# A two-layer hybrid decoder trunk on one core: weight blocks in tiles of 1024 columns instead of 512

## The chip, the cores and the metric

The kernel runs on one core of one Trainium2 chip. Its metric is the device time of one execution in microseconds (us), taken as the median of several runs. A core has TensorE for matrix products (PE in the rows, its weight loads PEld), VectorE (DVE), ScalarE (ACT), GpSimd (POOL) and SyncE (SP), which here issues all transfers between the chip's memory (HBM) and SBUF. Each engine works through its own instructions in the order in which the program lists them, and waits where an operand or a buffer isn't ready.

## The reference

The sequence has 512 tokens of width 1024, in float32; the trunk has two layers, each with three residual steps.

```python
for l in range(DEPTH):
    ff = swiglu(rms_norm(x, g[l, 0]), ffn_w1[l, 0], ffn_w3[l, 0], ffn_w2[l, 0])   # D_FF = 2816
    x = x + 0.5 * rms_norm(ff, g[l, 1])
    h = rms_norm(x, g[l, 2])
    p = h @ w_in[l]                       # 3336 columns (and 32 of w_in_vres in layer 1)
    y_a = rwkv7_time_mix(p[..., :1024])   # delta rule, 4 heads of 64
    y_b = s5_mix(p[..., 1024:1280])       # complex diagonal state space
    y_c = gated_deltanet_mix(p[..., 1280:3336])   # delta rule, 4 heads of 128
    x = x + rms_norm(concat(y_a, y_b, y_c) @ w_out[l], g[l, 3])
    ff = swiglu(rms_norm(x, g[l, 4]), ffn_w1[l, 1], ffn_w3[l, 1], ffn_w2[l, 1])
    x = x + 0.5 * rms_norm(ff, g[l, 5])
```

Here `swiglu(z, w1, w3, w2)` is `(silu(z @ w1) * (z @ w3)) @ w2`.

## The kernel before

The tokens are worked in two halves of 256. A list of steps in `run` names the stages: `A` and `B` are the two feed-forward networks, `P` the input projection, `M` the token mixers, `O` the output projection, followed by the layer and the half (`B10` is the second network of layer 1 on the first half); small letters begin a stage early or finish it late. A mixer of one half (`M`) is written next to a feed-forward stage of the other half, and a scheduler that works from a model of the engines' times decides how the instructions of neighbouring stages are interleaved on each engine. The order is fixed when the program is built.

Matrix products with weights are done to nearly float32 precision with fp32r operands: the activations and the weights are each split in a high part (a rounded copy) and a low part (the rest), and three products are added (`mm3`, lines 245 to 247). So each weight takes this path: a transfer by SP into a tile `raw`, a copy by ACT into `whi` (line 226), a subtraction by DVE into `wlo` (line 227), and then matmuls. A *block* is 1024 columns of weights on 128 partitions (512 KB): the 8 x 128 columns of one step of `w1`, `w3` or `w_in`, or 2 x 512 columns of one step of `w2` or `w_out`. `weight` takes a block in two tiles of 512 columns; `raw` has 6 buffers, `whi` and `wlo` have 4 each. The last columns of `w_in` (`gate`) come in four blocks of 2 x 520 (layer 0) or 2 x 552 columns (layer 1), a tile for each of the two.

A feed-forward step `f` of 22 (`up`, then `down` of the step before) uses a block of `w1` and one of `w3`, 24 matmuls of 256 columns each into the tile `ph`, and a block of `w2`, 12 matmuls of 512 columns into `acc`. A tile of 512 columns thus feeds 12 or 6 matmuls. Some `w_out` blocks (`plain` in `outmul`) are not split: TensorE reads them from `raw` in float32 (line 1355). The gains of the norms after a stage (`gain`) also use `raw` buffers, two per norm, from their transfer to the products at line 338.

At the start of a stage `prenorm` scales the rows into `xs` (line 299), TensorE turns them (`xt`, line 309), and for each of 8 slices of 128 columns ACT writes `hth` and DVE writes `htl` (lines 317 and 318), which the first matmuls of the stage need slice by slice. The mixers use small transfers on the same SP queue: `lv` and `lx` (lines 1243 and 1285) are the tables of the S5 mixer, and `scr` and `blk` (lines 568 and 571) rearrange the matrices to be inverted.

Of the kernel before, what the change touches and what calls it, by code (L numbers as in the profile page):

```python
# [12 lines left out]
F32 = mybir.dt.float32  # L13
F32R = mybir.dt.float32r
# [6 lines left out]
P = 128  # L21
# [20 lines left out]
class Trunk:  # L42
# [171 lines left out]
    def weight(self, src, n, w, src2=None, w2=0):  # L214

        nc = self.nc
        m = n // 2
        his, los = [], []
        for z in range(2):
            q = self.wts.tile([P, m, w + w2], F32, tag="raw", name=self.n("raw"), bufs=6)  # L220
            nc.sync.dma_start(out=q[:, :, 0:w], in_=src[:, z * m:z * m + m])
            if w2:
                nc.sync.dma_start(out=q[:, :, w:w + w2], in_=src2[:, z * m:z * m + m])
            hi = self.wts.tile([P, m, w + w2], F32R, tag="whi", name=self.n("whi"), bufs=4)
            lo = self.wts.tile([P, m, w + w2], F32R, tag="wlo", name=self.n("wlo"), bufs=4)
            nc.scalar.activation(hi, q, AF.Copy)  # L226
            nc.vector.tensor_tensor(lo, q, hi.bitcast(F32), ALU.subtract)  # L227
            his.append(hi)
            los.append(lo)
        return [his[k // m][:, k % m] for k in range(n)], [los[k // m][:, k % m] for k in range(n)]  # L230
# [93 lines left out]
    def postnorm(self, accs, h, gain, half, chunks=(0, 1)):  # L324
        with self.tc.high_priority(100):
            self.postnorm_(accs, h, gain, half, chunks)

    def postnorm_(self, accs, h, gain, half, chunks):
        nc = self.nc
        for i in chunks:  # L330
            x = self.x[2 * h + i]
            ss = self.sm([P, 2], "pss")
            for d in range(2):
                junk = self.fw.tile([P, 512], BF16, tag="junk", name=self.n("junk"), bufs=1)
                nc.scalar.activation(junk, accs[i][d], AF.Square, scale=(2.0 if half else 1.0) * D ** -0.5, accum_out=ss[:, d:d + 1])
            r = self.rstd2(ss, (4.0 if half else 1.0) * EPS, "po")
            for d in range(2):
                nc.vector.tensor_tensor(accs[i][d], accs[i][d], gain[d], ALU.mult)
            for d in range(2):
                e = slice(d * 512, (d + 1) * 512)  # L340
                nc.vector.scalar_tensor_tensor(x[:, e], accs[i][d], r, x[:, e], ALU.mult, ALU.add)

    def gain(self, l, i):
        ts = []
        for d in range(2):
            t = self.wts.tile([P, 512], F32, tag="raw", name=self.n("gain"), bufs=6)
            self.nc.sync.dma_start(out=t, in_=self.io["norm_gain"][l, i][d * 512:(d + 1) * 512].partition_broadcast(P))
            ts.append(t)
        return ts


    def up(self, S, f):
# [981 lines left out]
    def outmul(self, l, k, mixT, plain, chunks, accs):  # L1334

        nc = self.nc
        e = slice(chunks[0] * P, (chunks[-1] + 1) * P)
        src = self.io["w_out"][l][k * P:(k + 1) * P, :].rearrange("p (d e) -> p d e", d=2)
        if plain:
            ws = []  # L1340
            for d in range(2):
                w = self.wts.tile([P, 512], F32, tag="raw", name=self.n("raw"), bufs=6)
                nc.sync.dma_start(out=w, in_=src[:, d])
                ws.append(w)
        else:
            a = self.fw.tile([P, HALF], F32R, tag="gh", name=self.n("mh"), bufs=2)
            b = self.fw.tile([P, HALF], F32R, tag="gl", name=self.n("ml"), bufs=2)
            nc.scalar.activation(a[:, e], mixT[:, k, e], AF.Copy)
            nc.vector.tensor_tensor(b[:, e], mixT[:, k, e], a[:, e].bitcast(F32), ALU.subtract)
            wh, wl = self.weight(src, 2, 512)  # L1350
        for i in chunks:
            s = slice(i * P, (i + 1) * P)
            for d in range(2):
                if plain:
                    nc.tensor.matmul(accs[i][d], mixT[:, k, s], ws[d], start=k == 0, stop=k == KT - 1)  # L1355
                else:
                    self.mm3(accs[i][d], a[:, s], b[:, s], wh[d], wl[d], k == 0, k == KT - 1)
# [120 lines left out]

# [9 lines left out]
```

## Time and profile before

| | |
|---|---|
| median of 3 runs | 2284.42 us (2283.87 to 2288.77) |
| the profiled execution, its own time | 2297.84 us |
| its span, first to last instruction | 2296.1 us |
| TensorE busy with matmuls | 2235.3 us, 97% of the span |
| VectorE busy | 1686.1 us, 73% |
| ScalarE busy | 1190.5 us, 52% |
| GpSimd busy | 173.8 us, 8% |
| mean granted clock of TensorE | 0.988 |

A span is what the profiler saw between the first and the last instruction; the execution's own time is a little longer. Busy time is the union of an engine's instructions; an engine that is busy nearly all of the span sets the time, and what the others do matters where it makes that engine wait. The granted clock is 1.00 at 2.4 GHz and 0.50 at 1.2 GHz.

### The profile page before, as it was taken

The page shows a single profiled execution, that of the slowest core. Times are in us where ns is not written, and L with a number is a line of the kernel's source. Part 1 is how long each engine was busy: PE and PEld are TensorE (multiplying, and loading weights), DVE is VectorE, ACT ScalarE, POOL GpSimd, SP SyncE. Part 2 cuts the span into 40 slices and gives each one's busy share as a digit, 9 for nine tenths or more (in the row PEclk, how much of TensorE's full clock was granted, in tenths as well). Part 3 has the DMA queues.
Part 4 walks back from the last instruction along what each step waited for, and adds up shares of the span by engine and source line. Part 5 has one row for each costly group of instructions (what it writes and reads, how often), then busy time and mean ns, then how long its engine had stood idle before and what let it go on. Part 6 is the DMA issues. An engine that isn't in the chain of part 4 may idle for free.

```text
span 2296.1 us, 44446 instructions
## 1 busy us (share of the span) xinstructions
PE 2235.3 (97%) x15800; PEld 2048.1 (89%) x15800; DVE 1686.1 (73%) x3771; ACT 1190.5 (52%) x2513; POOL 173.8 (8%) x380
## 2 busy tenths in 40 slices
PE   8999999999999999999999999999999999999998
PEld 7998999997978999799999999899978889987997
DVE  6597885966877866859776688686777678667665
ACT  5455754444645544655555566445455444445554
POOL 2032000001100000202200010000010000001000
PEclk9999999999999999999999999999999899999999
DMA  6776755646756644576666676475477366445665
GB/s 205 192 209 188 190 164 159 201 142 176 186 160 185 192 136 148 170 204 206 200 178 188 187 195 169 127 214 161 143 195 200 107 193 187 137 126 182 189 186 155
DMA packets 604963, 403.67 MB, mean 176 GB/s; under 512 B 63306, under 2 KB 534340, under 8 KB 604740
## 3 DMA queue, kind: packets, MB, share of 16 engines
q1 hardware_dynamic: 604740, 400.82, 60.8%
q8 instruction: 124, 2.03, 0.4%
q14 instruction: 99, 0.81, 0.1%
HBM read 387.09 MB, written 13.63 MB: 175 GB/s over the span
## 4 chain that ended last, share of the span: by engine, by line
PE 87%; DMA 4%; DVE 4%; POOL 2%; issue 2%; ACT 1%; SPq 0%; DVEq 0%; ACTq 0%; POOLq 0%
PE ph L246 13%; PE ph L247 13%; PE ph L245 13%; PE acc L245 7%; PE acc L246 7%; PE acc L247 7%; PE pp L247 4%; PE pp L245 4%; PE pp L246 4%; PE acc L1355 1%; POOL Q L1196 1%; DVE wlo L227 1%; DMA raw<-in_w_out 1%; PE pk L760 1%; PE pb L764 1%
## 5 line engine op out<-in xcount | busy, mean ns | idle before, releaser
L226 ACT ACTIVATE whi<-raw 128x512 fp32r<-128x512 f32 (+2 forms) x1296 | 813.4, 632 | 857.4 <-PE ph L246 407.8
L227 DVE TENSOR_TENSOR wlo<-raw,whi 128x512 fp32r<-128x512 f32 (+2 forms) x1296 | 892.2, 692 | 427.0 <-ACT whi L226 408.9
L245 PE MATMUL ph<-hth,whi 128*128 128x256 f32 x2464 | 702.5, 285 | 6.8 <-DVE htl L318 2.9
L247 PE MATMUL ph<-hth,wlo 128*128 128x256 f32 x2464 | 703.5, 286 | 4.3 <-DVE wlo L227 4.1
L246 PE MATMUL ph<-htl,whi 128*128 128x256 f32 x2464 | 703.7, 286 | 2.0 <-DVE htl L318 1.8
L245 PEld LDWEIGHTS ph<-hth,whi 128*128 128x128 f32 x2464 | 468.1, 190 | 20.9 <-issue 5.5
L246 PEld LDWEIGHTS ph<-htl,whi 128*128 128x128 f32 x2464 | 467.2, 190 | 14.9 <-issue 3.9
L247 PEld LDWEIGHTS ph<-hth,wlo 128*128 128x128 f32 x2464 | 468.2, 190 | 11.5 <-DVE wlo L227 7.1
L246 PE MATMUL acc<-wlo,gh 128*128 128x512 f32 x704 | 277.3, 400 | 0.0
L247 PE MATMUL acc<-whi,gl 128*128 128x512 f32 x704 | 270.0, 397 | 0.3 <-DVE gl L371 0.3
L245 PE MATMUL acc<-whi,gh 128*128 128x512 f32 x704 | 257.4, 401 | 0.1
L247 PEld LDWEIGHTS acc<-whi,gl 128*128 128x128 f32 x704 | 132.0, 189 | 29.6 <-issue 0.7
L246 PEld LDWEIGHTS acc<-wlo,gh 128*128 128x128 f32 x704 | 132.4, 189 | 23.5 <-issue 1.0
L245 PEld LDWEIGHTS acc<-whi,gh 128*128 128x128 f32 x704 | 130.6, 190 | 22.7 <-issue 1.0
L370 ACT ACTIVATE gh<-gu 128x256 fp32r<-128x256 f32 x176 | 71.7, 407 | 58.6 <-DVE gu L364 57.7
L245 PE MATMUL pp<-hth,whi 128*128 128x256 f32 x352 | 99.6, 283 | 2.5 <-ACT whi L226 2.1
L245 PE MATMUL ph<-hx,whi 128*128 128x256 f32 x352 | 99.7, 283 | 0.9 <-DVE gu L364 0.9
L246 PE MATMUL ph<-hx,whi 128*128 128x256 f32 x352 | 99.5, 283 | 0.0
L247 PE MATMUL ph<-hx,wlo 128*128 128x256 f32 x352 | 99.4, 282 | 0.0
L247 PE MATMUL pp<-hth,wlo 128*128 128x256 f32 x352 | 98.7, 282 | 0.7 <-DVE wlo L227 0.7
L246 PE MATMUL pp<-htl,whi 128*128 128x256 f32 x352 | 98.6, 281 | 0.1
L245 PE MATMUL pp<-hx,whi 128*128 128x256 f32 x352 | 98.5, 281 | 0.0
(491 smaller groups left out, 3400.4 us busy)
## 6 DMA issues: line engine op xcount, KB each, us to landing
raw<-in_ffn_w SPq DMA_DIRECT2D x1056, 256.0 KB
raw<-in_w_in SPq DMA_DIRECT2D x176, 256.0 KB
raw<-in_w_out SPq DMA_DIRECT2D x96, 256.0 KB
raw<-in_w_in SPq DMA_DIRECT2D x32, 260.0 KB
gain<-in_norm_gain SPq DMA_DIRECT2D x28, 256.0 KB
lx<-s5w SPq DMA_DIRECT2D x16, 384.0 KB
lv<-s5w SPq DMA_DIRECT2D x16, 256.0 KB
x<-in_x SPq DMA_DIRECT2D x4, 512.0 KB
```

Of the source, the lines that this page charges most:

```text
L226: nc.scalar.activation(hi, q, AF.Copy)
L227: nc.vector.tensor_tensor(lo, q, hi.bitcast(F32), ALU.subtract)
L245: mm(out, lh, rh, start=start, stop=False)
L246: mm(out, lh, rl, start=False, stop=False)
L247: mm(out, ll, rh, start=False, stop=stop)
L370: nc.scalar.activation(gh, u, AF.Copy, scale=0.5)
L760: nc.tensor.matmul(pk[:, j], ka[q, j, c], ar[q, j, c], start=True, stop=True)
L764: nc.tensor.matmul(pb[:, j], be[q, j, c], ar[q, j, c], start=True, stop=True)
L1196: nc.gpsimd.tensor_scalar(Q[z][hp][q, :, j, 16 * g:16 * g + 16], cur[z][q, 4 * hp:4 * hp + 4], 1.0 - 2 * z, 0.0, ALU.mult, ALU.add)
L1355: nc.tensor.matmul(accs[i][d], mixT[:, k, s], ws[d], start=k == 0, stop=k == KT - 1)
```

## The change

`weight` takes a block of up to 1024 columns as one tile, with one transfer, one copy and one subtraction, instead of two of each. `raw` gets 5 tiles of 1024 columns (before 6 of 512), `whi` and `wlo` 3 each (before 4 of 512). Blocks of `gate` have more than 1024 columns and are still halved; each half of 520 or 552 columns then takes a whole buffer. The gain of a norm and a plain block of `w_out` become one tile with one transfer. A scratch area that the program reserves in SBUF for descriptors of transfers is set to 1024 bytes; no transfer of this kernel is issued by GpSimd.

```diff
     def weight(self, src, n, w, src2=None, w2=0):
...
-        m = n // 2
+        m = n if n * (w + w2) <= 1024 else n // 2
         his, los = [], []
-        for z in range(2):
-            q = self.wts.tile([P, m, w + w2], F32, tag="raw", name=self.n("raw"), bufs=6)
+        for z in range(n // m):
+            q = self.wts.tile([P, m, w + w2], F32, tag="raw", name=self.n("raw"), bufs=5)
             nc.sync.dma_start(out=q[:, :, 0:w], in_=src[:, z * m:z * m + m])
             if w2:
                 nc.sync.dma_start(out=q[:, :, w:w + w2], in_=src2[:, z * m:z * m + m])
-            hi = self.wts.tile([P, m, w + w2], F32R, tag="whi", name=self.n("whi"), bufs=4)
-            lo = self.wts.tile([P, m, w + w2], F32R, tag="wlo", name=self.n("wlo"), bufs=4)
+            hi = self.wts.tile([P, m, w + w2], F32R, tag="whi", name=self.n("whi"), bufs=3)
+            lo = self.wts.tile([P, m, w + w2], F32R, tag="wlo", name=self.n("wlo"), bufs=3)
             nc.scalar.activation(hi, q, AF.Copy)
             nc.vector.tensor_tensor(lo, q, hi.bitcast(F32), ALU.subtract)
...
     def gain(self, l, i):
-        ts = []
-        for d in range(2):
-            t = self.wts.tile([P, 512], F32, tag="raw", name=self.n("gain"), bufs=6)
-            self.nc.sync.dma_start(out=t, in_=self.io["norm_gain"][l, i][d * 512:(d + 1) * 512].partition_broadcast(P))
-            ts.append(t)
-        return ts
+        t = self.wts.tile([P, 2, 512], F32, tag="raw", name=self.n("gain"), bufs=5)
+        self.nc.sync.dma_start(out=t, in_=self.io["norm_gain"][l, i].rearrange("(d e) -> d e", d=2).partition_broadcast(P))
+        return [t[:, d] for d in range(2)]
...
         if plain:
-            ws = []
-            for d in range(2):
-                w = self.wts.tile([P, 512], F32, tag="raw", name=self.n("raw"), bufs=6)
-                nc.sync.dma_start(out=w, in_=src[:, d])
-                ws.append(w)
+            w = self.wts.tile([P, 2, 512], F32, tag="raw", name=self.n("raw"), bufs=5)
+            nc.sync.dma_start(out=w, in_=src)
+            ws = [w[:, d] for d in range(2)]
...
-    nc = bacc.Bacc("TRN2", target_bir_lowering=False, num_devices=1)
+    nc = bacc.Bacc("TRN2", target_bir_lowering=False, num_devices=1, dynamic_dma_scratch_size=1024)
```

The scheduler orders the engines anew. Three places show how.

The first is TensorE at the start of stage `B10`, 1793 us into the profile of before, where the turned rows (`hth`, `htl`) arrive slice by slice while the mixer `M11` (`pv`, `ptn`) begins. Before:

```order
L729 MATMUL pv_23923<-vr_23846,wv_3062_13558 128x256 x2
L747 MATMUL ptn_23935<-ident,be_23553 128x128 x2
L246 MATMUL ph_24752<-htl_23874,whi_24755 128x256
L247 MATMUL ph_24752<-hth_23873,wlo_24756 128x256
L747 MATMUL ptn_23939<-ident,ka_23554 128x128 x2
L245 MATMUL ph_24752<-hth_23877,whi_24755 128x256
L246 MATMUL ph_24752<-htl_23878,whi_24755 128x256
```

And of the change:

```order
L726 MATMUL pv_20885<-vr_20808,wv_2214_11862 128x256 x2
L744 MATMUL ptn_20897<-ident,be_20537 128x128 x2
L246 MATMUL ph_21714<-htl_20836,whi_21717 128x256
L247 MATMUL ph_21714<-hth_20835,wlo_21718 128x256
L246 MATMUL ph_21784<-htl_20836,whi_21787 128x256
L247 MATMUL ph_21784<-hth_20835,wlo_21788 128x256
L245 MATMUL ph_21714<-hth_20839,whi_21717 128x256
L245 MATMUL ph_21784<-hth_20839,whi_21787 128x256
L246 MATMUL ph_21714<-htl_20840,whi_21717 128x256
L247 MATMUL ph_21714<-hth_20839,wlo_21718 128x256
```

Before, each slice feeds one tile `ph` (step 0); now it feeds two (steps 0 and 1 of the feed-forward network), so twice the matmuls follow each slice.

The second is the SP queue at the end of the plain part of `O10`, 1765 us into the profile of before. Before:

```order
L1343 DMA raw_23645<-in_w_out 128x512
L1343 DMA raw_23647<-in_w_out 128x512
L347 DMA gain_23651<-in_norm_gain 128x512
L347 DMA gain_23653<-in_norm_gain 128x512
L221 DMA raw_23674<-in_w_in 128x520
```

And of the change:

```order
L1338 DMA raw_20607<-in_w_out 128x1024
L1338 DMA raw_20611<-in_w_out 128x1024
L345 DMA gain_20615<-in_norm_gain 128x1024
L221 DMA raw_20636<-in_w_in 128x520
L223 DMA raw_20636<-in_w_in_vres 128x32
```

The transfers come in the same order. The last block of `w_out` and the gain took four of six buffers ahead of the gate's first tile; now they take two of five.

The third is the SP queue in the mixer `M11`, 1853 us into the profile of before, at the transfers of `lv`. Before:

```order
L1243 DMA lv_5483_24273<-s5w_126 128x2x256
L221 DMA raw_25263<-in_ffn_w 128x4x128
L221 DMA raw_25269<-in_ffn_w 128x4x128
L568 DMA scr_24171<-ATg_24123 32x8x32 x4
L1243 DMA lv_5484_24279<-s5w_126 128x2x256
L221 DMA raw_25299<-in_ffn_w 128x4x128
L571 DMA blk_24180<-scr_24171 64x1024
L1243 DMA lv_5485_24285<-s5w_126 128x2x256
```

And of the change:

```order
L1240 DMA lv_3964_21235<-s5w_126 128x2x256
L221 DMA raw_22259<-in_ffn_w 128x8x128
L221 DMA raw_22298<-in_ffn_w 128x1024
L565 DMA scr_21133<-ATg_21085 32x8x32 x4
L1240 DMA lv_3965_21241<-s5w_126 128x2x256
L221 DMA raw_22317<-in_ffn_w 128x8x128
L568 DMA blk_21142<-scr_21133 64x1024
L1240 DMA lv_3966_21247<-s5w_126 128x2x256
```

The same number of weight transfers stands between the small ones, each now of twice the bytes.

## Rows read from the trace of the kernel before

**Rows 1.** The page: busy us (share of the span) and instructions of each engine.

```profile
PE 2235.3 (97%) x15800; PEld 2048.1 (89%) x15800; DVE 1686.1 (73%) x3771; ACT 1190.5 (52%) x2513; POOL 173.8 (8%) x380
```

**Rows 2.** Windows: length, busy us (instructions) of each engine, clock, DMA share, GB/s.

```profile
1200.00:1250.00 50.00, 50.00 (x356) 46.77 (x356) 30.82 (x55) 26.24 (x48) 0.00 (x0) 1.00 0.65 188
1777.40:1780.70 3.30, 3.30 (x16) 2.98 (x14) 3.30 (x7) 1.80 (x3) 0.92 (x2) 0.50 0.67 162
2112.00:2115.20 3.20, 3.20 (x12) 2.72 (x12) 1.24 (x3) 0.94 (x2) 0.00 (x0) 0.50 0.69 204
1797.90:1814.80 16.90, 16.90 (x53) 12.46 (x54) 8.17 (x28) 4.03 (x9) 0.00 (x0) 0.50 0.06 16
```

**Rows 3.** Who TensorE waited for: us in total, times, longest.

```profile
PE xt L309 <- DVE xs L299: 5.1, 3, 2.9
PE pto L1032 <- DVE og L1029: 5.0, 2, 4.5
PE ph L247 <- DVE wlo L227: 4.1, 7, 1.4
PE v L1246 <- DMA lv<-s5w: 3.6, 3, 1.8
PE pg L245 <- ACT whi L226: 3.4, 2, 1.9
PE ph L245 <- DVE htl L318: 2.9, 2, 2.7
PE pp L245 <- ACT whi L226: 2.1, 3, 1.2
PE ph L245 <- ACT gt L361: 2.0, 1, 2.0
PE ph L246 <- DVE htl L318: 1.8, 3, 1.2
PE y L1288 <- DMA lx<-s5w: 1.1, 2, 0.7
```

**Rows 4.** Groups by form: count, busy us, mean ns, idle before and its causes.

```profile
L227 DVE TENSOR_TENSOR wlo<-raw,whi 128x512 fp32r<-128x512 f32 x1264 | 869.8, 692 | 421.7 <-ACT whi L226 403.8 <-DMA raw<-in_ffn_w 6.2 <-PE ph L247 2.8
L226 ACT ACTIVATE whi<-raw 128x512 fp32r<-128x512 f32 x1264 | 792.8, 631 | 839.4 <-PE ph L246 407.8 <-PE acc L247 150.3 <-DVE wlo L227 57.9
L226 ACT ACTIVATE whi<-raw 128x552 fp32r<-128x552 f32 x16 | 10.4, 661 | 8.3 <-PE pg L247 3.8 <-DMA raw<-in_w_in_vres 2.5 <-DMA s5u<-us 0.7
L597 DVE TENSOR_TENSOR xb<-xc,bd 128x1024 f32<-128x1024 f32 x8 | 9.6, 1201 | 0.0
```

**Rows 5.** Timeline of the start: start, length, engine, instruction.

```profile
6.77 0.63 ACT L226 ACTIVATE whi<-raw 128x512 fp32r<-128x512 f32 x1 [0.18 <-DMA raw<-in_ffn_w]
7.68 0.63 ACT L226 ACTIVATE whi<-raw 128x512 fp32r<-128x512 f32 x1 [0.28 <-DMA raw<-in_ffn_w]
8.58 0.88 DVE L299 TENSOR_SCALAR xs<-x,pnr 128x512 f32<-128x512 f32 x2 [0.46 <-POOL pnr L269]
11.18 0.48 DVE L318 SCALAR_TENSOR_TENSOR htl<-xt,pg,hth 128x256 fp32r<-128x256 f32 x1
12.21 0.88 DVE L318 SCALAR_TENSOR_TENSOR htl<-xt,pg,hth 128x256 fp32r<-128x256 f32 x2 [0.54 <-ACT hth L317]
```

**Rows 6.** The chain that ended last, pieces in order of time: start, length, what.

```profile
1766.54 0.23 PE acc L247
...
1858.29 0.12 PE ph L245
...
1862.87 5.40 DMA lv<-s5w
```

**Rows 7.** Timeline around two waits of TensorE, at 1868 and 2110 us.

```profile
1868.31 1.10 PE L1246 MATMUL v<-U,lv 128*128 128x64 f32 x8 [1.79 <-DMA lv<-s5w]
...
2108.93 0.63 ACT L226 ACTIVATE whi<-raw 128x512 fp32r<-128x512 f32 x1 [2.44 <-DMA raw<-in_ffn_w]
...
2110.26 0.37 ACT L361 ACTIVATE gt<-ph 128x256 f32<-128x256 f32 x1
```

## Prediction

> **What bounds the kernel now.** I read the page first, then the windows of 50 us, the waits of TensorE, and the timeline at its longest waits. On the page TensorE is busy for 2235.3 us, 97% of the span of 2296.1 us [rows 1]. The windows show what a full stretch looks like, here one of a feed-forward stage: 50.00 of 50 us and 356 matmuls, with VectorE at 30.82 us and ScalarE at 26.24 [rows 2]. There TensorE alone sets the time: a feed-forward step is 48 matmuls at 0.12 us and 12 at 0.23 us [rows 6], 8.5 us, whatever happens to the weights before. So a gain can only come from the places where TensorE waits: 2296.1 - 2235.3 = 60.8 us, and the time behind a wait at which its clock is 0.50, that is 1.2 GHz. The waits view tells what ended them [rows 3]. Some concern the weights (`whi`, `wlo`, `raw`), some the start of a stage (`xs`, `htl`), some the mixers (`og`, `lv`, `lx`).
>
> The profiled execution took 2297.84 us, 13.4 us more than the median of 2284.42. I sum differences against the profiled one and apply them to the median.
>
> **The copies and subtractions.** Of 1264 tiles of 512 columns [rows 4], 632 remain with 1024. VectorE: the trace has an elementwise product of 1024 columns at 1201 ns, against 2 x 692 ns for two subtractions [rows 4], so 0.183 us less per block, 116 us in all. ScalarE: no copy of 1024 columns is there. From 512 to 552 columns it grows by 30 ns, 0.75 ns a column [rows 4], which gives 631 + 384 = 1015 ns; without any saving it is 2 x 631 = 1262 ns. I take 1015, since the shapes are those of this very line: 0.247 us per block, 156 us in all (0 at the other end). I cost both savings at nothing directly, because both engines have idle time in the full windows: the cover is TensorE's own work, and only in a stretch where VectorE is full would up to 0.18 us a block show.
>
> **The ring of split tiles.** Before, a tile fed 12 matmuls of `ph`, 1.4 us; four tiles are 5.6 us of work in hand. Now a tile feeds 24, 2.8 us, and three are 8.4 us. A freed buffer is refilled by a copy and a subtraction: 0.63 + 0.69 = 1.3 us before, under three tiles of cover (4.2 us); now 1.02 (to 1.26) + 1.20 = 2.2 to 2.5 us, under two tiles (5.6 us). So the full stretches stay full: zero, and if that cover failed, each block would cost up to the 2.5 us. `raw` holds 5 x 512 KB instead of 6 x 256 KB, so 1 MB more of weights can wait in SBUF.
>
> **Term A, waits for weights.** `ph` on `wlo` 4.1, `pg` on `whi` 3.4 and `pp` on `whi` 2.1 us [rows 3]; smaller ones I leave out. One more belongs here: the 2.0 us for `gt` at 2110, since that activation stood on ScalarE behind copies that had waited 2.44 us for a transfer [rows 3, 7]. Behind this wait and behind both waits at the gate the clock is 0.50 for some 3.3 us (the rows show two of the three stretches) [rows 2], half of which is lost, 3 x 1.65 = 4.9 us. Ceiling: 11.6 + 4.9 = 16.5 us. The waits at the gate (3.4 us and two stretches, 6.7 us) I leave out: the gate's tiles keep their size and come behind the same bytes of `w_out` and of the gain in the queue; the buffers left beside these are three of five instead of two of six, but `whi` and `wlo` have one less. The remaining 9.8 us are single waits of at most 2 us, and the ring is 2.8 us deeper; I take three quarters, **-7.4 us** (bounds 0 and -16.5).
>
> **Term B, starts of stages.** Where slices arrive one by one, the order of before gives TensorE three matmuls a slice, 0.36 us, while slices come about 0.7 us apart (two `htl` from 12.21, one at 11.18) [rows 5]. At `B10` that is followed by 16.9 us at clock 0.50 with only 53 matmuls, 8.4 us lost [rows 2]. The new order feeds two steps from each slice, 0.7 us. Ceiling: 8.4 + 2.9 + 1.8 (waits for `htl`, [rows 3]) = 13.1 us. The mixer's own short float32 matmuls stand there too, and don't get denser; I take half, **-6.6 us** (bounds 0 and -13.1).
>
> **Terms that cost.** C: small transfers queue behind loads that are twice as large. 256 KB of weights land 0.91 us apart (copies that waited for them start at 6.77 and 7.68) [rows 5]. TensorE waited for `lv` three times and for `lx` twice [rows 3]; if each stands 256 KB further back, 5 x 0.91 = 4.6 us; I take **+2**, as some have no load just ahead (bounds 0 and 4.6). D: at the start two subtractions of 1.20 us now stand between `xs`, which ends at 8.58 + 0.88 = 9.46, and the first `htl`, so 11.9 instead of 11.18, and a third before the second `htl`, 13.6 instead of 12.21 [rows 5]; two steps per slice make part of it good: **+0.7** (bounds 0 and 1.4). E: an operation of the mixers or of the norm that finds VectorE in a subtraction waits up to 0.51 us longer; five waits on `xs` and `og` were exposed [rows 3]: **+1** (bounds 0 and 2.5). Plain `w_out` blocks and gains become one transfer for two, which costs nothing by itself: the issues on SP lie beside TensorE's work, and a late landing would stand in the waits above. The scratch area is used by no instruction of the trace: nothing.
>
> Sum: -7.4 - 6.6 + 2 + 0.7 + 1 = -10.3 us. Against the profiled execution that is 2297.8 - 10.3 = 2287.5; against the median 2284.4 - 10.3 = **2274 us**.
>
> **Rivals.** *No change* (2280 to 2289): the weights' waits move to the next late thing. Where a `whi` comes earlier, the transfers of a mixer or the products on VectorE end the wait instead, since the mixers' chains are as long as before. For it: single waits on weights are short and spread (7 times for 4.1 us). Against it: in the full windows nothing else is late. A and B then give about 3 us, C to E take them back.
>
> *Slower*: the SP queue of the mixers. In `M11` two weight tiles stand ahead of `scr` and the next `lv`, and one more ahead of `blk`, each now 256 KB larger: 3 x 0.91 = 2.7 us later in each of four mixers, 11 us. The `lv` transfer of 1862.87 took 5.40 us until it had landed, and TensorE waited 1.79 us for it [rows 6, 7]. It decides from the point at which the mixer's chain, not the feed-forward matmuls beside it, ends last; at 5.0 us for `og` [rows 3] that point is reached at the end of a mixer. With E and D at their upper ends and A at a third, 11 + 2.5 + 1.4 - 5.5 = +9: 2294 us. The Trainium skill, "DMA: Bandwidth & Descriptors", section "Queues, rings and completion order", says that on each DMA engine the descriptors of one issuing queue are consumed in ring order; by that, every small transfer on SP pays for all weights issued ahead of it, and this rival is the result. The 5.40 us of `lv` agree with it.
>
> *Larger gain*: all waits for weights and the half-clock stretches go, 16.5 + 13.1 = 30 us: 2255 us. The Trainium skill, "TensorE: Matmul & The Clock Gate", Part 1, says that the slow clock is the default and activity releases it; by that each wait that goes also gives back a slow stretch, as in A.
>
> **Numbers.** The forecast has a chance of 0.52, the larger gain 0.12, no change 0.18, slower 0.18. A measurement of this kernel tells about 0.2% (4.6 us) from no change. Most of the forecast and all of the larger gain are faster: 0.62; the edge of the forecast and the rival give 0.20 for the same; 0.18 slower. With A and B at zero and C to E at their ends (+8.5) the time is 2293, with the opposite ends 2255; the slower rival lies at 2294, so the range is 2252 to 2294 us, with 3 us below for what VectorE's freed time may add, and the forecast's own is 2263 to 2280.
>
> **What would show it.** Right: some 632 subtractions of about 1.2 us; waits of `ph`, `pp` and `acc` on `whi` and `wlo` below 3 us in all; no long half-clock stretch at the start of `B10`; windows in the feed-forward stages still at 50.00 with about 356 matmuls. C would show as waits for `lv`, `lx` and `og` above 10 us. Wrong: a subtraction well over 1.2 us, full windows with fewer matmuls, or a new half-clock stretch behind a mixer.

## The result, and the profile after

The changed kernel takes 2324.53 us (median of 4 runs, 2322.86 to 2328.06), the kernel before 2286.60 us beside it (4 runs, 2283.87 to 2289.23): a ratio of 1.0146, 95% interval 1.0115 to 1.0177. It is slower by 38 us. I had forecast 2274, with a range that ended at 2294.

The page of the changed kernel, busy time of each engine:

```profile
span 2321.7 us, 40638 instructions
...
PE 2236.4 (96%) x15800; PEld 2059.6 (89%) x15800; DVE 1620.9 (70%) x3139; ACT 1077.0 (46%) x1881; POOL 187.0 (8%) x380
```

VectorE and ScalarE are freed by 65 and 114 us against [rows 1], and the time is longer. The copies and subtractions, by form (count, busy us, mean ns, idle before and its causes), answer to [rows 4]:

```profile
L227 DVE TENSOR_TENSOR wlo<-raw,whi 128x1024 fp32r<-128x1024 f32 x632 | 773.3, 1225 | 465.1 <-ACT whi L226 455.3 <-PE pnq L919 2.3 <-DMA raw<-in_ffn_w 1.6
L226 ACT ACTIVATE whi<-raw 128x1024 fp32r<-128x1024 f32 x632 | 668.9, 1059 | 860.7 <-PE ph L246 343.9 <-issue 208.3 <-PE acc L247 200.1
```

632 of each, at 1225 and 1059 ns, where I had 1201 and 1015. Who TensorE waited for, to be read against [rows 3]:

```profile
PE pto L1029 <- DVE og L1026: 12.0, 4, 4.9
PE xt L309 <- DVE xs L299: 8.0, 5, 2.8
...
PE pty L848 <- DVE y L845: 5.1, 1, 5.1
...
PE pg L246 <- DVE wlo L227: 4.4, 4, 2.2
...
PE acc L245 <- ACT gh L367: 2.8, 3, 1.5
...
PE acc L246 <- DVE wlo L227: 2.1, 1, 2.1
PE ph L245 <- ACT whi L226: 2.0, 2, 1.1
...
PE y L1285 <- DMA lx<-s5w: 1.7, 2, 1.4
PE pp L247 <- DVE wlo L227: 1.5, 2, 1.0
PE v L1243 <- DMA lv<-s5w: 1.4, 2, 1.2
...
PE pp L245 <- ACT whi L226: 0.6, 1, 0.6
...
PE pg L245 <- ACT whi L226: 0.4, 1, 0.4
```

The waits for `lv` and `lx` fell from 4.7 to 3.1 us. Those for split weights (`whi` and `wlo`) come to 11.0 us in these six rows; before, with the small rows that [rows 3] leaves out, to 12.0. What grew most is the mixers' late operations, `og` (5.0 to 12.0, of which the 4.5 at the end of `M11` were there before) and `y` (not among the rows before, now 5.1), and `xs`, which opens a stage (5.1 to 8.0): 15.0 us together, of 24.5 us by which TensorE is idle longer (85.3 for 60.8). The rest is spread over small rows. The windows say the same by stage (length, busy us of the engines, clock, DMA share, GB/s):

```profile
1250.00:1300.00 50.00, 50.00 (x360) 47.23 (x360) 28.59 (x36) 22.30 (x31) 0.00 (x0) 1.00 0.63 189
...
900.00:950.00 50.00, 43.69 (x262) 36.76 (x260) 33.66 (x64) 20.20 (x46) 8.13 (x16) 0.93 0.37 125
...
2050.00:2100.00 50.00, 39.68 (x240) 35.43 (x240) 27.05 (x52) 17.82 (x34) 2.96 (x6) 0.90 0.31 105
```

And the last two windows before:

```profile
900.00:950.00 50.00, 47.52 (x254) 37.52 (x253) 36.41 (x73) 28.33 (x68) 7.26 (x14) 1.00 0.50 156
...
2050.00:2100.00 50.00, 41.52 (x189) 33.93 (x188) 32.44 (x62) 25.65 (x62) 6.73 (x12) 0.90 0.41 127
```

A full stretch is as full as before. These thin ones lie at the ends of mixers (`M01` and `M11`), and the second was nearly as thin before. The end of `M00` shows how it comes about. In the changed kernel, on TensorE, `g` of line 1011 is the last step of the mixer's chain on this engine before `pto`; `pp` are matmuls of the projection of the other half, which need nothing from it:

```profile
596.31 1.05 PE L1011 MATMUL g<-vt,AQg 128*128 128x128 f32 x8
602.28 0.91 PE L1029 MATMUL pto<-ident,og 128*128 128x128 f32 x3 [4.92 <-DVE og L1026]
602.84 0.56 PE L245 MATMUL pp<-hth,whi 128*128 128x256 f32 x1
```

The same two steps in the order of before, from the profile of e10 (below), a second look at that order:

```profile
578.59 1.05 PE L1014 MATMUL g<-vt,AQg 128*128 128x128 f32 x8
...
587.28 0.60 PE L1032 MATMUL pto<-ident,og 128*128 128x128 f32 x4
```

A window of e10 between them, with TensorE's busy time and instructions, clock, DMA share and GB/s:

```profile
579.64:587.28 7.64, 7.64 (x68) 1.00 0.46 114
```

And the last products of `og` there, on VectorE:

```profile
584.73 1.14 DVE L1029 SCALAR_TENSOR_TENSOR og<-og,onr,gw 128x128 f32<-128x128 f32 x4
```

In the order of before, matmuls of `pp` fill the 7.64 us between the two steps. VectorE and ScalarE have `og` ready at 584.73 + 1.14 = 585.87, 6.2 us after `g`, so `pto` finds it ready. Now no `pp` stands there: TensorE takes its instructions in order, the `pp` matmuls stand behind `pto`, and it is idle for 4.92 us. The mixer's chain itself took no more time than before. The wait goes on costing behind itself, since the clock is then 0.50, with 22 matmuls in 4.55 us (a window of the changed kernel, all engines):

```profile
602.28:606.83 4.55, 4.55 (x22) 4.45 (x23) 3.98 (x11) 1.91 (x6) 0.00 (x0) 0.50 0.03 8
```

The Trainium skill, "TensorE: Matmul & The Clock Gate", Part 1, says that the slow clock is the default and activity releases it; these rows agree, with 0.50 behind 4.92 us without a matmul.

### The profile page after: what moved, and what is told of

Same layout as the page of the kernel before. It is cut to its first block, busy times and chain, and to the rows that moved or that the text cites. A ratio compares the mean times of both kernels' runs of the same rounds, so it can differ in the third digit from the quotient of the medians.

```text
span 2321.7 us, 40638 instructions
## 1 busy us (share of the span) xinstructions
PE 2236.4 (96%) x15800; PEld 2059.6 (89%) x15800; DVE 1620.9 (70%) x3139; ACT 1077.0 (46%) x1881; POOL 187.0 (8%) x380
## 5 line engine op out<-in xcount | busy, mean ns | idle before, releaser
L227 DVE TENSOR_TENSOR wlo<-raw,whi 128x1024 fp32r<-128x1024 f32 (+2 forms) x664 | 795.8, 1200 | 485.1 <-ACT whi L226 475.1
L226 ACT ACTIVATE whi<-raw 128x1024 fp32r<-128x1024 f32 (+2 forms) x664 | 689.4, 1040 | 892.0 <-PE ph L246 343.9
L245 PEld LDWEIGHTS ph<-hth,whi 128*128 128x128 f32 x2464 | 472.9, 192 | 15.8 <-ACT whi L226 2.4
L246 PEld LDWEIGHTS ph<-htl,whi 128*128 128x128 f32 x2464 | 474.2, 192 | 14.2 <-DVE htl L318 4.2
L247 PEld LDWEIGHTS ph<-hth,wlo 128*128 128x128 f32 x2464 | 474.3, 192 | 5.6 <-issue 3.0
L245 PE MATMUL acc<-whi,gh 128*128 128x512 f32 x704 | 271.2, 396 | 2.8 <-ACT gh L367 2.8
```

Source lines behind the costliest of these rows:

```text
L245: mm(out, lh, rh, start=start, stop=False)
L246: mm(out, lh, rl, start=False, stop=False)
L247: mm(out, ll, rh, start=False, stop=stop)
```

## The experiments

Three ways of holding an order are used, all of them rules for the scheduler that leave every wait as it is. *Held on TensorE*: its 14,792 instructions, numbered as the program writes them (the trace counts 15,800 matmuls), follow each other as in a list that was read off another kernel:

```diff
+    pe = [i for i in nc.cur_bb.bb.instructions if str(i.engine) == "EngineType.PE"]
+    for a, b in zip(order, order[1:]):
+        tc.add_manual_dep(pe[b], pe[a].name, DependencyInfo(NoSync, SCHED_ONLY), reason="order")
```

*Held on all engines*: the same for TensorE, VectorE, ScalarE, GpSimd and SP, where the two halves of a block count as one. *Mixers held*: only pairs, a mixer's instruction and the feed-forward matmuls that may not stand ahead of it. Ratios are against before on the same chip, with 95% intervals; its median there lies between 2289.91 and 2297.38 us, so across these runs ratios compare better than times.

**e1 and e2, the two tiles in each other's order of TensorE.**

```diff
# e1: the changed kernel, TensorE in the order of before
- raw bufs=5, whi bufs=3, wlo bufs=3
+ raw bufs=3, whi bufs=4, wlo bufs=4
# e2: the kernel before, TensorE in the order of the change
- raw bufs=6, whi bufs=4, wlo bufs=4
+ raw bufs=9, whi bufs=6, wlo bufs=6
```

> Tiles of 1024 columns as in the change (3 raw, 4 high, 4 low, the same bytes), but TensorE's 14,792 instructions are held in the order of the kernel before. Theory *order* (the loss is where the scheduler put TensorE's instructions once more split weights were in hand: feed-forward matmuls stand further ahead of the mixers' chains, whose ends are then exposed): 2276 to 2292 us, within 0.3% of before or faster. Theory *long operations* (subtractions of 1.2 us and copies of 1.04 us stand before the mixers' and norms' own operations): 2310 to 2325 us, most of the loss stays.

> The other cell: tiles of 512 columns as before, with the ring in bytes about that of the change (9 raw, 6 high, 6 low), and TensorE held in the order of the changed kernel. *Order*: 2312 to 2330 us, the loss comes with the order although every copy and subtraction is short. *Long operations*: 2280 to 2295 us.

e1: 2390.71 us, 1.0410 (1.0377 to 1.0444). e2: 2340.70 us, 1.0189 (1.0159 to 1.0220). The order of the change is slow with the old tiles too, as the order theory has it (1.9%, and 1.5% for the change); but the old order with the new tiles is slower still, which it does not.

**e3 and e4, the ring's depth, order left to the scheduler** (e3: the kernel before with 9, 6 and 6 tiles; e4: the change with 3, 2 and 2).

> Tiles of 512 columns with the deeper ring (9 raw, 6 high, 6 low), scratch of 1 KB, order left to the scheduler. If the *order* theory holds and the depth of the ring is what moves the order: 2300 to 2325 us. If the order moves for the size of the tiles and not for the depth: 2280 to 2295. *Long operations*: 2276 to 2288, as no operation is longer and more weights are in hand.

> Tiles of 1024 columns with the bytes of before (3 raw, 2 high, 2 low), order left to the scheduler. *Order*, with depth as its cause: 2285 to 2305 us, less than the change loses, what remains being waits for weights, since one tile must be refilled (2.3 us) under the 2.8 us of the other. *Long operations*: 2318 to 2335 us.

e3: 2306.42 us, 1.0063 (1.0039 to 1.0087). e4: 2359.86 us, 1.0286 (1.0257 to 1.0315). With a deeper ring, and the order that the scheduler writes for it, the kernel before is slower, not faster. In e4 `ph` waited 21.9 us for `wlo`, in 23 waits: it is above both its ranges, two tiles are too few, and it says little of the order.

**e5 and e6, the change with its mixers held** on TensorE, 4 and 2 us.

```diff
+        held(nc, tc)   # tc.add_manual_dep(pe[filler], pe[mixer].name, ..., reason="order")
```

> The changed kernel as it is (5 raw, 3 high, 3 low tiles of 1024), with one rule more for the scheduler: on TensorE, feed-forward and projection matmuls may stand at most some 4 us of work further ahead of a mixer's instruction than in the kernel before. Nothing is pinned otherwise. Theory *order* (the feed-forward matmuls run out before the mixer's chain ends): the losses at the ends of the four mixers go, 20 to 32 us, so 2290 to 2305 us. Theory *tile size* (1024 columns cost by themselves, as in e1): 2318 to 2340 us.

> As e5 with 2 us in place of 4. *Order*: as e5 or up to 6 us faster, 2284 to 2303 us. *Tile size*: 2318 to 2345 us. If holding the mixers makes matmuls wait for something else, it is slower than e5.

e5: 2342.68 us, 1.0201 (1.0173 to 1.0229). e6: 2319.40 us, 1.0109 (1.0069 to 1.0150). The *order* theory misses both times; *tile size* gives the time of e6, and e5 is slower still. TensorE's waits in e6:

```profile
PE pp L247 <- DVE htl L320: 6.5, 2, 3.6
...
PE py L609 <- DVE xb L596: 6.0, 3, 3.4
...
PE pto L1031 <- DVE og L1028: 4.5, 1, 4.5
```

The ends of the mixers are repaired (`og` 12.0 to 4.5), and other waits, for `htl` and `xb`, have come in their place. So the exposed ends are where the loss shows, not all of what makes it.

**e7, e8 and e9, length of operations and transfers.** TensorE in the order of the change in e7 and e8; e9 is e6 with the halves of e7.

```diff
# e7, e9
-            nc.scalar.activation(hi, q, AF.Copy)
-            nc.vector.tensor_tensor(lo, q, hi.bitcast(F32), ALU.subtract)
+            for c in (slice(0, m // 2), slice(m // 2, m)):
+                nc.scalar.activation(hi[:, c], q[:, c], AF.Copy)
+                nc.vector.tensor_tensor(lo[:, c], q[:, c], hi[:, c].bitcast(F32), ALU.subtract)
# e8: the same loop around the transfer of q
```

> The changed kernel with TensorE held in its own order, and each copy and each subtraction of 1024 columns done as two of 512; tiles and transfers stay. *Order*: 2316 to 2330 us, as the changed kernel. *Long operations* (term E of the prediction, mis-sized): a mixer's operation waits at most 0.69 us again, so most of the loss goes, 2290 to 2305 us.

> The changed kernel with TensorE held in its own order, and each transfer of 512 KB done as two of 256 KB; tiles, copies and subtractions stay. *Order*: 2316 to 2330 us. *Large transfers* (term C and the slower rival): the small transfers of the mixers come earlier and the loss goes by 8 to 11 us, 2308 to 2316 us.

> The changed kernel with the mixers held on TensorE as in e6 (2 us), and each copy and subtraction of 1024 columns done as two of 512. Neither alone gave the loss back (e6 +1.1%, e7 +1.2%). Theory *both* (a subtraction of 1.2 us lengthens the mixers' chains, and the order of the change hides that inside the mixers and shows it at their ends, so each edit alone only moves the exposure): 0.0 to +0.6% against before. Theory *tiles* (something of the large tiles that neither the order nor the operations' length makes, such as the ring's unit): +0.9 to +1.3%, as e6.

e7: 2322.65 us, 1.0121 (1.0093 to 1.0148). e8: 2332.96 us, 1.0164 (1.0139 to 1.0189). e9: 2349.61 us, 1.0256 (1.0222 to 1.0290). Neither the long subtractions nor the long transfers carry the loss in this order of TensorE, and the theory *both* falls with e9, which is above the range of *tiles* too. That e9 is 1.5% above e6 with shorter operations suggests how much an order that is written anew can move by itself; the other engines of e7 and e8, and most of e9, are free to be ordered anew.

**e10, the scratch area alone.**

```diff
-    nc = bacc.Bacc("TRN2", target_bir_lowering=False, num_devices=1)
+    nc = bacc.Bacc("TRN2", target_bir_lowering=False, num_devices=1, dynamic_dma_scratch_size=1024)
```

> The kernel before with a scratch area of 1 KB alone. All theories: 0.0%, within 0.2%. Its profile is a second look at the order of before: if the stretch of 16.9 us at half clock at the start of B10 belongs to that order, it is there again; if it belongs to the one execution that was profiled (13 us over the median), it is gone, and with it most of what term B of the prediction meant to gain.

2287.02 us, 0.9987 (0.9960 to 1.0013): nothing, as expected. TensorE's order is that of before. Its page:

```profile
span 2283.3 us, 44446 instructions
...
PE 2222.4 (97%) x15800; PEld 2037.9 (89%) x15800; DVE 1686.7 (74%) x3771; ACT 1190.6 (52%) x2513; POOL 174.2 (8%) x380
```

And its windows at the start of `B10`, all engines:

```profile
1795.00:1800.00 5.00, 4.49 (x22) 3.00 (x21) 4.16 (x16) 2.56 (x8) 0.00 (x0) 1.00 0.00 0
1800.00:1805.00 5.00, 5.00 (x33) 4.04 (x31) 4.25 (x15) 1.73 (x4) 0.00 (x0) 1.00 0.20 56
```

In e10 TensorE comes 2.2 us earlier to the same place, so its windows from 1795 answer to the stretch from 1797.90 before. The clock there is 1.00, and 55 matmuls run in 10 us, where the profiled execution of before had 53 in 16.9 us at 0.50 [rows 2]. So the stretch doesn't come with the order each time. How often it comes is open: the 56 executions of before that ran beside the experiments took 2282 to 2304 us, 12 of them 2297 or more, so the profiled one, at 2297.84, was no rare one.

Against the profile of e10 the change has 38.4 us more span, as much as between the medians: 24.4 us more of idle TensorE (85.3 for 60.9) and 14.0 us more busy for the same 15,800 matmuls. Against the first profile of before it is 24.5 us more of idle time again, but only 1.1 us more busy.

**e11 and e12, two cross-checks**: e3 with the mixers held as in e6, and e1 with the halves of e7.

> e3 (tiles of 512 columns, 9 raw, 6 high, 6 low) with the mixers held on TensorE as in e6 (2 us). e3 alone was +0.6%, its losses at the ends of mixers (about 6 us each at the ends of M00, M01 and M11). *Order* or *both*: the ends are given back and the short operations keep the mixers' chains as they were, -0.6 to +0.2%. If the mixers' positions are not what costs in e3: +0.4 to +0.8%.

> e1 (tiles of 1024 columns, 3 raw, 4 high, 4 low, TensorE in the order of before; +4.1%) with each copy and subtraction done as two of 512. *Both*: most of e1's loss goes, +0.5 to +2%. *Tiles*: the transfers of 512 KB into three buffers and the tiles freed whole keep e1 late, +3 to +4.2%.

e11: 2314.18 us, 1.0095 (1.0070 to 1.0120). e12: 2380.45 us, 1.0378 (1.0350 to 1.0406). Holding the mixers doesn't help the old tiles either (e11 is above both ranges), and most of e1's loss is not the length of its operations.

**e13 and e14, all five engines held**, tiles as in e2 and e1.

> Tiles of 512 columns (9 raw, 6 high, 6 low), with the instructions of all five engines held in the order of the changed kernel; the two halves of a block follow each other where the change has one instruction. *Order* (all engines): +1.1 to +1.9% against before, as the change. *Tiles*: -0.4 to +0.4%.

> Tiles of 1024 columns (3 raw, 4 high, 4 low, the bytes of before), with all five engines held in the order of before; a block's one transfer, copy and subtraction stand where the first of its two halves stood. *Order*: -0.3 to +0.5% (a subtraction that stands where its first half stood is 0.5 us longer there and 0.7 us less later). *Tiles*: +2.5 to +4.2%, as e1 and e12.

e13: 2334.62 us, 1.0200 (1.0173 to 1.0227). e14: 2361.70 us, 1.0316 (1.0292 to 1.0339). TensorE's waits in e13, tiles of 512 columns:

```profile
PE pto L1043 <- DVE og L1040: 11.7, 4, 4.9
PE xt L319 <- DVE xs L309: 8.5, 4, 3.3
...
PE pg L256 <- DVE wlo L231: 4.4, 4, 2.2
PE pty L862 <- DVE y L859: 4.2, 1, 4.2
```

These are nearly the change's own waits (`og` 12.0 in 4, `xs` 8.0 in 5, `pg` 4.4 in 4, `y` 5.1 in one), without its tiles; a longer one for `lx` (8.2 us in all) is e13's own. The loss comes with the order, TensorE's above all, since e2 holds that alone and loses 1.9%. The new tiles add nothing to it: the change, with the same order, loses 1.5%. And e14 says that the old order is no way out for the new tiles, at least with three raw ones.

**e15 and e16, small changes of the ring** (e15: before with 5 high and 5 low tiles; e16: the change with 4 raw tiles), order left to the scheduler.

> The kernel before with 5 high and 5 low tiles in place of 4 (scratch 1 KB), order left to the scheduler. More buffers cannot hurt where the order stays: -0.2 to 0.0%. If any new order costs, because the one of before is an exceptionally good one: +0.3 to +1.0%.

> The changed kernel with 4 raw tiles in place of 5, order left to the scheduler. TensorE's order is nearly that of the change (positions differ by 1.4 instructions on average, 11.6 between before and the change). *Order*: +1.2 to +1.9%, as the change; if transfers issued further ahead were what hurts: +0.5 to +1.1%.

e15: 2285.98 us, 0.9982 (0.9964 to 1.0000). e16: 2318.51 us, 1.0132 (1.0109 to 1.0155). TensorE's order in the trace of e15 is another than that of before. So not every new order costs, and the fifth raw tile isn't what hurts.

**e17 and e18, which unit makes the old order slow.** All engines in the order of before. e17 has raw tiles and transfers of 1024 columns alone, e18 high and low tiles of 1024 alone.

```diff
# e17: one transfer, two copies and subtractions into tiles of 512
+            if z == 0: q = self.wts.tile([P, n, w + w2], F32, tag="raw", bufs=3); nc.sync.dma_start(out=q[:, :, 0:w], in_=src)
+            c = q[:, z * m:z * m + m]
# e18: two transfers, copies and subtractions, into one tile of 1024
+            if z == 0: hw, lw = (tiles [P, n, w + w2], tags "whi" and "wlo", bufs=4)
+            hi, lo = hw[:, z * m:z * m + m], lw[:, z * m:z * m + m]
```

> All five engines in the order of before; raw tiles and transfers of 1024 columns (3, the bytes of before), but copies, subtractions and split tiles of 512 columns as before (4 high, 4 low). If the unit of *raw tiles and transfers* is what loses in e14 (a copy of 512 columns waits until 512 KB have landed, and 512 KB come free at a time): +2.0 to +3.2%. Otherwise -0.3 to +0.6%.

> All five engines in the order of before; high and low tiles of 1024 columns (4 each, twice the bytes of before), filled by copies and subtractions of 512 columns from raw tiles and transfers of 512 columns as before (6). If the unit in which *split tiles* come free is what loses in e14: +2.0 to +3.2%. Otherwise -0.4 to +0.4%, as there are even more bytes. If e17 and e18 are both near zero, the *length of copies and subtractions* at the places of the old order is left.

e17: 2370.25 us, 1.0347 (1.0309 to 1.0384). e18: 2285.11 us, 0.9972 (0.9950 to 0.9994). e17 alone is as slow as e14. What ScalarE waited for in e17 (us in total, times, longest):

```profile
ACT whi L233 <- DMA raw<-in_ffn_w: 59.5, 38, 4.9
...
ACT whi L233 <- DMA raw<-in_w_in: 23.6, 14, 3.7
...
ACT whi L233 <- DMA raw<-in_w_out: 14.5, 5, 4.7
...
ACT whi L233 <- DMA raw<-in_w_in_vres: 10.0, 8, 2.1
```

One of these waits on ScalarE's timeline of e17:

```profile
649.01 0.63 ACT L233 ACTIVATE whi<-raw 128x512 fp32r<-128x512 f32 x1 [4.74 <-DMA raw<-in_w_out]
649.55 0.40 ACT L520 ACTIVATE ct<-cv 128x256 f32<-128x256 f32 x1
```

The same waits of ScalarE in the order of before with transfers of 256 KB (e10):

```profile
ACT whi L226 <- DMA raw<-in_ffn_w: 23.1, 22, 3.2
...
ACT whi L226 <- DMA raw<-in_w_out: 9.1, 6, 2.9
ACT whi L226 <- DMA raw<-in_w_in: 8.9, 9, 2.5
ACT whi L226 <- DMA raw<-in_w_in_vres: 2.5, 3, 1.5
```

ScalarE stood 107.6 us for weights that had not landed, for 43.6 before. A copy that waits holds up what is queued behind it on its engine: at 649 the copy waited 4.74 us, and an operation of a mixer, `ct`, follows it at once. But the sum of these waits is not the cost, for in e18 they come to 87.6 us, most of them here:

```profile
ACT whi L233 <- DMA raw<-in_ffn_w: 63.9, 72, 3.0
```

The large high and low tiles do no harm; with twice the bytes e18 is slightly faster than before, with the lowest ratio of these runs, though not clear of e10's. There the copies have more buffers and get ahead of TensorE, so that their waits don't reach it. What costs in e17 is what reaches TensorE:

```profile
PE pp L258 <- ACT whi L233: 9.6, 6, 3.2
PE acc L258 <- ACT whi L233: 5.5, 5, 1.7
```

With its smaller rows TensorE waited 21.0 us for `whi` in e17, 6.1 in e10 and 5.9 in e18. That is 14.9 of the 37.7 us by which it is idle longer than in e10; the rest is spread over other waits, among them `lv` and `lx` (9.6 us for 5.4), and isn't taken apart here. e17 changes the raw tile and the transfer together, so it doesn't say which of the two it is; in the order of the change, halving the transfers alone gained nothing (e8).

## Why the prediction was wrong

**The step that failed.** The sum took each stage as it stood and let only single waits come and go; the order of the engines entered it at the starts of stages alone (term B). No term priced where the scheduler puts the mixers' steps among the feed-forward and projection matmuls over a whole mixer; that stood at nothing without a reason. It is what the change moved, and e13 shows its price with the old tiles: 2.0%, with nearly the same waits. The rival on the slower side had the wrong mechanism: in the change the engines wait less for the mixers' transfers, TensorE for `lv` and `lx`, and VectorE for `blk`, first before and then in the change:

```profile
DVE tmp L579 <- DMA blk<-scr: 16.4, 4, 5.3
...
DVE tmp L576 <- DMA blk<-scr: 7.8, 4, 2.9
```

**Copies, subtractions, the ring.** Right in kind: 632 of each at 1225 and 1059 ns, full windows still at 50.00, and freed time on VectorE and ScalarE that buys nothing. The savings by their rows are 97 and 124 us, where I had 116 and 156.

**Term A** (-7.4). Right in part, but not in the sum. Behind the first 40 us, `ph` and `acc` wait next to nothing for `whi` and `wlo`, and `pp` 2.1 us; before, the three waited 7.4 us there. The 2.0 us for `gt` are gone, but `gh` now takes 2.8. In the first 40 us they wait 4.1 us instead of 1.2, and the gate (`pg`) waits 4.8 us for 3.4. So `ph`, `pp` and `acc` stand at 6.2 us in all, above the 3 that I had named, and all waits for split weights at 11.0 for 12.0.

**Term B** (-6.6). The stretch at half clock was in the one profiled execution and is not in e10, in the same order. I took it for the kernel's habit, priced it against an execution 13.4 us above the median and took the gain off the median. In the executions that make the median there was little of it to gain.

**Term C** (+2). `lv` and `lx` 3.1 us for 4.7: no cost. The sign that I had named for it (`lv`, `lx` and `og` above 10 us) came all the same, with 15.1, but 12.0 of them are `og`, which is VectorE's. The new half-clock stretch behind a mixer, a sign of being wrong, came too, at 602.28.

**Term D** (+0.7). Too small, though the places are right: the first two `htl` start at 12.03 and 13.83, where I had 11.9 and 13.6. TensorE from 8 to 40 us in the changed kernel (busy, instructions, clock, DMA share, GB/s):

```profile
8.00:40.00 32.00, 27.49 (x178) 1.00 0.67 202
```

And in e10, then in the first profile of before:

```profile
8.00:40.00 32.00, 30.60 (x208) 1.00 0.67 200
...
8.00:40.00 32.00, 29.71 (x198) 1.00 0.65 190
```

It is idle 2.2 to 3.1 us longer and gets 20 to 30 matmuls less done. The waits there are for weights: 2.0 us of `ph` for `whi`, and one of 2.1 us of `acc` for the `wlo` of a block of `w2`. Two steps per slice need the second block's copy as well.

**Term E** (+1). Its waits, `xs` and `og`, grew by 9.9 us, ten times the term, and `y` added 5.1. The reason was not the 0.51 us by which a subtraction is longer: e7 has the short operations in the same order of TensorE, with 11.9 us for `og`, and is within the interval of the change.

**What stays open.** The experiments with all engines held separate order from tiles, but not why the scheduler wrote this order for 5 raw, 3 high and 3 low tiles. The ring of e13 is deeper than that of before, and that it does no harm in a held order is shown for the high and low tiles alone (e18). That the unit of raw tiles and transfers makes the old order slow is shown for three raw tiles (e17); with five it wasn't tried. And the ends of the mixers are not the whole loss, since e5 and e6 repair them and stay slow, and e16, with 5.6 us for `og`, still loses 1.3%.

## What to carry to other kernels

Where a scheduler decides, a new tile size is first of all a new order on every engine: hold the order on all engines and change the tile, then hold the tile and change the order, before a term of the sum is trusted. Look at how much independent work the new order leaves between the last steps of each long chain, since an in-order engine can't fetch it from behind the wait. Where the bytes of a ring stayed the same and the order was held, smaller tiles with transfers of their own did better here; a copy that waits for a large one also holds up all that is queued behind it. And look at a second profile of the same order before a stretch of the first is priced.

## What the runs showed of the hardware that I had not expected

A slow kernel can lose as much in clock as in waiting. In e17 TensorE is busy 2267.2 us for the work that takes 2222.4 in e10, 44.8 of the 82.5 us between their spans, at a mean granted clock of 0.974 for 0.995. In the change it is 14.0 of 38.4, at 0.986.

The granted clock differs from one execution to the next of the same program: in the ten executions of e10 it goes from 0.984 to 0.996, and the time from 2309 to 2282 us. The change lies at 0.985 to 0.987 in all four of its own.

Raw tiles and transfers of 512 KB instead of 256, with the same bytes of buffers and the same order, cost 3.5% (e17). The Trainium skill, "DMA: Bandwidth & Descriptors", section "Bandwidth", advises to batch transfers to 1 MiB or more for most of the peak rate. No run here goes that far, but the rate does improve from 256 to 512 KB: in e10 and then in e17, the same bytes on SP's queue (packets, MB, share of the span of 16 engines) take 61.0% of 2283.3 us and 57.5% of 2365.8, 2.3% less.

```profile
q1 hardware_dynamic: 604740, 400.82, 61.0%
...
q1 hardware_dynamic: 563428, 400.78, 57.5%
```

The kernel is slower all the same; among other things TensorE waits longer for `whi` (21.0 us for 6.1). A better rate of the transfers is not by itself a faster kernel.
